# States of the samples copied through DRAM scratch beside the pair products, transposed as fp32r, and updated into their own tile

## The chip, the cores and the metric

The kernel runs on one core of one Trainium2 chip. Its engines have separate instruction streams: TensorE (PE in the profile, its weight loads PEld), VectorE (DVE), ScalarE (ACT), GpSimd (POOL) and SyncE (SP). SP and ACT also issue DMAs; SP's are on queue q1 and ACT's on queue q10. The metric is the device time of one execution in microseconds (us); the time given is the median of several runs.

## What is computed

One layer of a hybrid decoder for a prompt of 1024 tokens and for 8 samples of 8 tokens each. A projection of the normalized input feeds a pooling branch and a state-space (SSD) branch; their outputs are gated, added and projected. The change concerns the SSD branch of the samples, where each of the 32 heads has a state of 64 x 128 from an earlier step:

```python
def step(h, inp):
    xq, dq, Bq, Cq = inp
    acs = jnp.cumsum(dq * Ag, axis=1)
    ...
    y = jnp.einsum('bijge,bjgep->bigep', att, xq)
    y = y + jnp.einsum('bign,bige,bgepn->bigep', Cq, jnp.exp(acs), h)
    last = acs[:, -1]
    w_in = jnp.exp(last[:, None] - acs) * dq
    h = h * jnp.exp(last)[..., None, None] + jnp.einsum('bjgn,bjge,bjgep->bgepn', Bq, w_in, xq)
    return h, y
```

For the samples there is one such step per sample. `h` (8 samples x 32 heads x 64 x 128, 8.4 MB in float32) is an input, `state_ssm`. It is used twice: in `y`, which needs it turned (the state dimension n on the partitions), and in the new `h`, which is an output.

## The kernel before

All 1088 tokens (1024 + 64) lie on the free axis, features on the 128 partitions. Products that need float32 accuracy are made of three fp32r products of high and low parts ("whi", "wlo" are the parts of a weight tile, made by ACT at L166 and by POOL or DVE at L169).

The program has five stages on the span. Up to about 100 us the input is normalized. From 100 to 585 us come the **pair products**: `pair` makes two blocks of 128 columns of the big projection at a time by seven Strassen products (lines L609 to L611 on PE), whose raw weights are loaded on SP into a ring of five tiles named rawA (L541, L544, in `pair_w`). Beside them `splits` prepares other weights: it loads them on ACT, halves them, and stores one half on SP (L442, tiles pw to DRAM ws or wp). From about 590 to 790 us the last ten pairs run with the **samples' SSD** beside them (`ssd_samples`, called by `samples_beside`, a generator whose steps are spread evenly over the products). From 800 to 1120 us the prompt's SSD runs in chunks, beside more products, and the last stage is the output projection.

In `ssd_samples`, for each of four groups g of eight heads, the states come in eight tiles h0 of [128, 4, 128]: two heads on the partitions, four samples on the free axis. They have a ring of four buffers (`H0B`). For each half hf of the samples and each q of 0 to 3:

- `h0_load` (L1239, SP) loads one tile from `state_ssm`, in pieces of 512 bytes, three tiles ahead;
- PE turns it in four transposes against the identity `ident` (L1304), and ACT copies the result out of PSUM (L1306);
- one step later `update` makes the product for the new state on PE (L1291), DVE computes the new state in four operations **in place, into h0** (L1294), and ACT's queue stores h0 to the output (L1296). So a buffer of h0 is free for the next load only when that store has landed.

Ahead of these, each group loads its decays (dec, L1188 on SP from the DRAM tensor acs_d), which POOL masks in two operations (`far`, L1196 and L1197) and ACT puts through an exponential (L1202). The names of tiles that the views show: h is h0; hst holds the samples' x, B, C and their factors E; dec is also the name of two operands of L1291.

Before the samples, `dt_end` turns the time steps: it loads two tiles s0 and s1 from dts_d (L1090, L1091, SP) and transposes them (L1109).

What sets the order: the program is written with generators, `behind(engine)` holds an instruction back behind the last one that stands on that engine, and a scheduler then sets each engine's order within what the data and the buffers allow. An engine works through its list in order; SP's DMAs too, so that one which waits for a buffer holds back all that stand behind it.

Of the kernel before, what the change touches and what calls it, by code (L numbers as in the profile page):

```python
# [8 lines left out]
F32 = mybir.dt.float32  # L9
# [11 lines left out]
P = 128  # L21
# [4 lines left out]
NS = 64  # L26
# [20 lines left out]
def tile_pool_ssd_step(  # L47
# [6 lines left out]
    nc = tc.nc  # L54
# [41 lines left out]
    def PB():  # L96
        return psB.tile([P, 512], F32, tag="ps", name=nm("ps"))
# [19 lines left out]
    def turn_r(out, src):  # L117
        nc.tensor.transpose(out.bitcast(F32R), src.bitcast(F32R), identR)
# [272 lines left out]
    def dram(name, shape, dt=F32):  # L391
        return dr.tile(list(shape), dt, tag=name, name=name)
# [13 lines left out]
    def behind(engine, n=0):  # L406

        of = (i for i in reversed(nc.cur_bb.bb.instructions) if i.engine == engine)
        for _ in range(n):
            next(of)  # L410
        return tc.issue_after(next(of))
# [665 lines left out]
    def dt_end():  # L1077
# [7 lines left out]
        for rr in range(3):  # L1085
            nc.gpsimd.tensor_copy(blk3[32 * rr:32 * rr + 32], blk[:32, 0:4])
        F = 9 * NH
        s0 = sp.tile([P, 8 * P], F32, tag="dec", name="s0", bufs=2)
        s1 = sp.tile([P, NS], F32, tag="bt", name="s1", bufs=2)
        load(s0, dts_d[:, :SEQ])  # L1090
        load(s1, dts_d[:, SEQ:])  # L1091
# [128 lines left out]
    def spt(shape, tag, bufs, dt=F32):  # L1220
        return sp.tile(list(shape), dt, tag=tag, name=nm(tag), bufs=bufs)

    def ssd_samples(g):
        S = NS
        xb = spt([P, 6, NS], "hst", 2)
        load(xb, xbc_d[g][:, :, SEQ:])
        Bf, Cf = xb[:, 4], xb[:, 5]
        E2 = spt([P, 4, NS], "hst", 2)
        load_E(E2, g)
        dec = spt([P, 8, P], "dec", 2)[:NS, :, :NS]  # L1230
        decays(dec, g, NC)
        far(dec, NC)
        exps(dec, g, NC)
        h0s = {}

        def h0_load(j):
            hf, q = divmod(j, 4)
            h0 = spt([P, 4, P], "h0", H0B)
            load(h0, state_ssm[0, 4 * hf:4 * hf + 4, 8 * g + 2 * q:8 * g + 2 * q + 2].rearrange("b h p n -> (h p) b n"))  # L1239
            h0s[j] = h0  # L1240
        h0_load(0)
        yield
        px = PB()
        for q in range(4):
            nc.tensor.transpose(px[:S, q * P:(q + 1) * P], xb[:, q], ident)
        pc = PB()
        mm(pc[:S, :S], Bf, Cf, start=True, stop=True)
        xd = spt([P, 8, 64], "xd", 2)
        V.tensor_tensor(xd[:S], px[:S].rearrange("p (h d) -> p h d", d=64),
                        dtT[:S, NC, 8 * g:8 * g + 8].unsqueeze(2).to_broadcast([S, 8, 64]), ALU.mult)  # L1250
        V.tensor_tensor(dec, dec, pc[:S, :S].unsqueeze(1).to_broadcast([S, 8, S]), ALU.mult)
        for j in range(1, H0B - 1):
            h0_load(j)
        yield
        t = spt([P, 4, P], "xd", 2)[:, :, :NS]
        for q in range(4):
            act(t[:, q], xb[:, q], AF.Copy, scale=Dv[:, 4 * g + q:4 * g + q + 1])
        yield
        V.tensor_tensor(t, inner(xd, dec, S), t, ALU.add)
        for hf in range(2):  # L1260
            rep = spt([P, 5, 2, 3, 16], "yt", 1).rearrange("p q a r i -> p q (a r i)").rearrange(
                "p q (r i) -> p q r i", i=32)
            nc.gpsimd.tensor_copy(rep, xb[:, 0:5, 32 * hf:32 * hf + 32].unsqueeze(2).to_broadcast([P, 5, 3, 32]))
            px = PB()
            for q in range(4):
                nc.tensor.transpose(px[:96, q * P:(q + 1) * P], rep[:, q].rearrange("p r i -> p (r i)"), ident)
            pb = PB()
            nc.tensor.transpose(pb[:96, :P], rep[:, 4].rearrange("p r i -> p (r i)"), ident)
            xs = spt([P, 8, 64], "xw", 1)
            V.tensor_tensor(xs[:96], px[:96].rearrange("p (h d) -> p h d", d=64),  # L1270
                            wd3[:, hf, 8 * g:8 * g + 8].unsqueeze(2).to_broadcast([96, 8, 64]), ALU.mult)
            xh = spt([P, 512], "dec", 2, F32R)
            xsf = xs.rearrange("p h d -> p (h d)")
            act(xh[:96], xsf[:96], AF.Copy)
            V.tensor_tensor(xh[64:96], xsf[64:96], xh[64:96].bitcast(F32), ALU.subtract)
            bx = spt([P, P], "bt", 2, F32R)
            act(bx[:96], pb[:96, :P], AF.Copy)
            V.tensor_tensor(bx[32:64], pb[32:64, :P], bx[32:64].bitcast(F32), ALU.subtract)
            Bb = spt([P, 4, P], "dec", 2, F32R)
            V.tensor_tensor(Bb[:96], bx[:96].bitcast(F32).unsqueeze(1).to_broadcast([96, 4, P]),  # L1280
                            blk3.unsqueeze(2).to_broadcast([96, 4, P]), ALU.mult)
            cz = spt([P, 4, 32], "cz", 2)
            V.memset(cz, 0.0)
            V.tensor_copy(cz[:, :, 0:8], Cf[:, 32 * hf:32 * hf + 32].rearrange("p (b i) -> p b i", i=8))
            yield
            hts = {}

            def update(r):
                h0 = h0s.pop(4 * hf + r)
                pu = PB()  # L1290
                mm(pu, xh[:96, r * P:(r + 1) * P], Bb[:96].rearrange("p b n -> p (b n)"), start=True, stop=True)  # L1291
                for b in range(4):
                    cc_ = 32 * hf + 8 * b + 7
                    V.scalar_tensor_tensor(h0[:, b, :], h0[:, b, :], E2[:, r, cc_:cc_ + 1],  # L1294
                                           pu[:, b * P:(b + 1) * P], ALU.mult, ALU.add)
                store_(new_ssm_s[0, 4 * hf:4 * hf + 4, 8 * g + 2 * r:8 * g + 2 * r + 2]  # L1296
                       .rearrange("b h p n -> (h p) b n"), h0)
            for q in range(4):
                j = 4 * hf + q
                if j + H0B - 1 < 8:  # L1300
                    h0_load(j + H0B - 1)
                pt = PB()
                for b in range(4):
                    nc.tensor.transpose(pt[:, b * P:(b + 1) * P], h0s[j][:, b, :], ident)  # L1304
                hts[q] = spt([P, 512], ("hT", "yt", "hU", "hV")[q], 1)
                act(hts[q], pt, AF.Copy)  # L1306
                if q > 0:
                    update(q - 1)
                yield
            po = PB()  # L1310
            for r in (3, 0, 1, 2):
                for b in range(4):
                    mm(po[32 * b:32 * b + 32, r * P:(r + 1) * P], cz[:, b, :], hts[r][:, b * P:(b + 1) * P],
                       start=True, stop=True)
            update(3)
            yo = spt([P, 512], "hT", 1)
            act(yo, po, AF.Copy)
            yield
            pn = PB()
            for q in range(4):  # L1320
                nc.tensor.transpose(pn[:, q * P:(q + 1) * P], yo[:, q * P:(q + 1) * P], ident)
            tn = spt([P, 4, P], "yt", 1)[:, :, :32]
            V.tensor_tensor(tn.rearrange("p q (b i) -> p q b i", i=8),
                            pn.rearrange("p (q b i) -> p q b i", q=4, i=32)[:, :, :, 0:8],
                            E2[:, :, 32 * hf:32 * hf + 32].rearrange("p q (b i) -> p q b i", i=8), ALU.mult)
            th = t[:, :, 32 * hf:32 * hf + 32]
            V.tensor_tensor(th, th, tn, ALU.add)
            yield
        store_(ys_d[g], t)
# [191 lines left out]
    def run_units(units, ahead=1, beside=None):  # L1521
        pend = {}
        widx = [i for i, u in enumerate(units) if u[0] is not None]
        nxt = 0
        done_w = 0
        for i, (pf, run) in enumerate(units):
            if pf is not None:
                while nxt < len(widx) and nxt <= done_w + ahead:
                    pend[widx[nxt]] = units[widx[nxt]][0]()
                    nxt += 1  # L1530
                done_w += 1
                it = run(pend.pop(i))
                for _ in it or ():
                    if beside is not None:
                        beside()
            else:
                run(None)
        while later:
            step()

    def plain(f):
        return (None, lambda w: f())
# [41 lines left out]
    units = [plain(to_conv), light[1], plain(pool_rows)]  # L1584
    units += weave(heavy, light[2:-LAST])
    pre = splits()
    units.append(plain(lambda: [None for _ in pre]))
    units.append(plain(to_ssd))
    acc = [None] * 8
    yh, yl = [None] * NG, [None] * NG  # L1590
    run_units(units, 1, lambda: next(pre, None))
    side = iter([it for g in range(NG) for it in [ssd_samples(g)] * SSTEPS])
    due, made_ = [0.0], [0]
    FIRST = 14
# [460 lines left out]
```

## Time and profile before

| | |
|---|---|
| median of three runs | 1273.08 us (1272.99 to 1273.53) |
| the profiled execution's own time | 1271.29 us |
| its span, first to last instruction | 1269.5 us |
| PE busy | 1242.3 us, 98% of the span |
| DVE, ACT, POOL busy | 900.9, 718.0, 683.1 us |
| moved by DMA | 234.9 MB, 185 GB/s over the span |

The profile is of one execution. A line such as "L1304 PE MATMUL ps<-ident,h 128*128 128x128 f32 x4" reads: line 1304 of the kernel, on PE, writes tile ps from ident and h, 4 times in a row. In a timeline the first two numbers are start and time in us, and a bracket at the end gives idle time before and what ended it. Matmuls overlap each other: a matmul's duration says little, the distance from one start to the next says what it costs PE.

### The profile page before, as it was taken

Reading aid. Unit: us, or ns where it says so; the run is one execution under the profiler, and the core shown is the slowest. Engines: PE = TensorE matmul, PEld = TensorE weight load, DVE = VectorE, ACT = ScalarE, POOL = GpSimd, SP = SyncE. Lnnn points to the kernel's source line nnn. Section 1 sums busy time; section 2 is a strip of 40 time slices with the busy share of each in tenths; the row PEclk is TensorE's granted clock in tenths of the full one; section 3 lists DMA queues with packets and bytes.
Section 4 is the critical chain, followed back from the end, with each engine's and each line's share of the span. In section 5 each row is a group of like instructions: output and inputs, shape, how many; then the busy total and the mean of one; then the engine's idle time right before and its main releaser. Section 6 shows DMA issues by size and latency. Waiting matters only on the chain. (4 is left out here: it accounts for less than half of the span.)

```text
span 1269.5 us, 26341 instructions
## 1 busy us (share of the span) xinstructions
PE 1242.3 (98%) x9771; PEld 1173.9 (92%) x9771; DVE 900.9 (71%) x1584; ACT 718.0 (57%) x1683; POOL 683.1 (54%) x555
## 2 busy tenths in 40 slices
PE   7999999999999999999999999999999999999997
PEld 6779999999999999998989999999999999999786
DVE  4695678966979588975756665598677879766543
ACT  4665356474666656554554554687887768522211
POOL 1007669886878777764344454365565646545000
PEclk9999999999999999999999999999999999999999
DMA  9937354565456454443557445899766567485431
GB/s 332 298 104 226 116 167 161 181 204 160 138 182 201 146 182 164 149 138 116 157 142 226 151 147 167 283 300 319 217 200 201 181 212 206 152 291 179 149 108 50
DMA packets 225729, 234.90 MB, mean 185 GB/s; under 512 B 30369, under 2 KB 177009, under 8 KB 225594
## 3 DMA queue, kind: packets, MB, share of 16 engines
q1 hardware_dynamic: 155808, 159.01, 40.3%
q10 hardware_dynamic: 69794, 74.22, 17.4%
q8 instruction: 77, 1.26, 0.4%
q14 instruction: 50, 0.41, 0.1%
HBM read 158.67 MB, written 74.62 MB: 184 GB/s over the span
## 5 line engine op out<-in xcount | busy, mean ns | idle before, releaser
L169 POOL TENSOR_TENSOR wlo<-rawA,whi 128x512 fp32r<-128x512 f32 x120 | 189.0, 1580 | 170.5 <-ACT whi L166 95.8
L169 POOL TENSOR_TENSOR wlo<-raw,whi 128x512 fp32r<-128x512 f32 x92 | 155.1, 1693 | 122.2 <-ACT whi L166 119.3
L360 PE MATMUL mm<-Y,whi 128*128 128x352 f32 (+1 forms) x480 | 159.8, 333 | 0.7
L361 PE MATMUL mm<-Y,whi 128*128 128x352 f32 (+1 forms) x480 | 157.3, 328 | 0.4 <-DVE Y L1516 0.4
L362 PE MATMUL mm<-Y,wlo 128*128 128x352 f32 (+1 forms) x480 | 156.8, 327 | 0.0
L609 PE MATMUL mm<-Y,whi 128*128 128x272 f32 x496 | 146.3, 295 | 2.2 <-ACT whi L166 2.2
L611 PE MATMUL mm<-Y,wlo 128*128 128x272 f32 x496 | 143.5, 290 | 2.5 <-POOL wlo L169 2.0
L609 PE MATMUL ps<-Y,whi 128*128 128x272 f32 x496 | 143.8, 290 | 0.0
L610 PE MATMUL ps<-Y,whi 128*128 128x272 f32 x496 | 143.0, 288 | 0.0
L610 PE MATMUL mm<-Y,whi 128*128 128x272 f32 x496 | 142.9, 288 | 0.0
L611 PE MATMUL ps<-Y,wlo 128*128 128x272 f32 x496 | 142.5, 287 | 0.0
L1057 DVE SCALAR_TENSOR_TENSOR GA<-GA,cvT,GA 128x1112 f32<-128x1112 f32 x72 | 126.6, 1763 | 0.1
L166 ACT ACTIVATE whi<-rawA 128x512 fp32r<-128x512 f32 x125 | 78.1, 627 | 81.1 <-PE ps L610 44.0
L166 ACT ACTIVATE whi<-raw 128x512 fp32r<-128x512 f32 x96 | 58.9, 627 | 97.6 <-DVE raw L555 51.7
L609 PEld LDWEIGHTS mm<-Y,whi 128*128 128x128 f32 x496 | 93.5, 189 | 4.2 <-ACT whi L166 2.8
L611 PEld LDWEIGHTS mm<-Y,wlo 128*128 128x128 f32 x496 | 93.5, 189 | 2.9 <-POOL wlo L169 2.2
L360 PEld LDWEIGHTS mm<-Y,whi 128*128 128x128 f32 x480 | 90.3, 188 | 4.2 <-DVE G L1890 2.4
L610 PEld LDWEIGHTS mm<-Y,whi 128*128 128x128 f32 x496 | 93.5, 189 | 0.7 <-issue 0.6
L610 PEld LDWEIGHTS ps<-Y,whi 128*128 128x128 f32 x496 | 93.3, 188 | 0.4
L609 PEld LDWEIGHTS ps<-Y,whi 128*128 128x128 f32 x496 | 93.3, 188 | 0.2
L611 PEld LDWEIGHTS ps<-Y,wlo 128*128 128x128 f32 x496 | 93.4, 188 | 0.0
L361 PEld LDWEIGHTS mm<-Y,whi 128*128 128x128 f32 x480 | 90.3, 188 | 2.6 <-DVE Y L1516 0.9
(464 smaller groups left out, 3821.9 us busy)
## 6 DMA issues: line engine op xcount, KB each, us to landing
rawA<-in_w_in SPq DMA_DIRECT2D x46, 512.0 KB
dec<-acs_d SPq DMA_DIRECT2D x32, 512.0 KB
xbc<-GA ACTq DMA_DIRECT2D x24, 512.0 KB
xb<-xbc SPq DMA_DIRECT2D x32, 384.0 KB
rawA<-in_w_in SPq DMA_DIRECT2D x32, 256.0 KB
pw<-in_w_ssm_out ACTq DMA_DIRECT2D x32, 256.0 KB
ws<-ph ACTq DMA_DIRECT2D x32, 256.0 KB
ws<-pw SPq DMA_DIRECT2D x32, 256.0 KB
```

The source lines that it names most:

```text
L166: ins = act(hi[:, :, :ncols], raw[:, :, :ncols], AF.Copy)
L169: (eng or nc.gpsimd).tensor_tensor(lo[:, :, :ncols], raw[:, :, :ncols], hi[:, :, :ncols].bitcast(F32), ALU.subtract)
L360: mm(ps[:, :n], a, rh[k][:, o:o + n], start=(k == 0), stop=False)
L361: mm(ps[:, :n], a, rl[k][:, o:o + n], start=False, stop=False)
L362: mm(ps[:, :n], b, rh[k][:, o:o + n], start=False, stop=(k == nk - 1))
L609: mm(p, hi, ah, start=(k == 0), stop=False)
L610: mm(p, hi, al, start=False, stop=False)
L611: mm(p, lo, ah, start=False, stop=(k == 3))
L1057: V.scalar_tensor_tensor(d[:, :n], rp[:, k:k + n], cvT[:, 24 * k + mc:24 * k + mc + 1], d[:, :n], ALU.mult, ALU.add)
```

## The change

Three things are done. The 32 tiles of the states are copied by 32 DMAs from `state_ssm` to DRAM scratch `h0_d`, already in the order of a tile h0, while the pair products run (one copy in every four steps); `h0_load` then reads the scratch, 2 KB per partition in one piece. The transposes are declared fp32r, by `turn_r`, which the prompt's SSD uses already (its instruction is L118). The new state is written to a tile hn of its own, with a ring of two buffers, and stored from there. To make room, dec becomes [128, 8, 64] in place of [128, 8, 128], and s0 of `dt_end` moves from the ring dec to the ring rawA.

```diff
-        s0 = sp.tile([P, 8 * P], F32, tag="dec", name="s0", bufs=2)
+        s0 = pa.tile([P, 8 * P], F32, tag="rawA", name="s0", bufs=5)
...
-        dec = spt([P, 8, P], "dec", 2)[:NS, :, :NS]
+        dec = spt([P, 8, NS], "dec", 2)[:NS]
...
             h0 = spt([P, 4, P], "h0", H0B)
-            load(h0, state_ssm[0, 4 * hf:4 * hf + 4, 8 * g + 2 * q:8 * g + 2 * q + 2].rearrange("b h p n -> (h p) b n"))
+            load(h0, h0_d[8 * g + j])
...
                 pu = PB()
+                hn = spt([P, 4, P], "hn", 2)
...
-                    V.scalar_tensor_tensor(h0[:, b, :], h0[:, b, :], E2[:, r, cc_:cc_ + 1],
+                    V.scalar_tensor_tensor(hn[:, b, :], h0[:, b, :], E2[:, r, cc_:cc_ + 1],
...
-                       .rearrange("b h p n -> (h p) b n"), h0)
+                       .rearrange("b h p n -> (h p) b n"), hn)
...
-                    nc.tensor.transpose(pt[:, b * P:(b + 1) * P], h0s[j][:, b, :], ident)
+                    turn_r(pt[:, b * P:(b + 1) * P], h0s[j][:, b, :])
...
+    h0_d = [dram(f"h0{n}", [P, 4, P]) for n in range(32)]
+
+    def move_states():
+        for n in range(32):
+            g, hf, q = n // 8, n // 4 % 2, n % 4
+            with behind(mybir.EngineType.SP):
+                load(h0_d[n], state_ssm[0, 4 * hf:4 * hf + 4, 8 * g + 2 * q:8 * g + 2 * q + 2].rearrange("b h p n -> (h p) b n"))
+            for _ in range(4):
+                yield
+    moved = move_states()
...
-    run_units(units, 1, lambda: next(pre, None))
+    run_units(units, 1, lambda: (next(pre, None), next(moved, None)))
```

How the order of instructions moves, at three places (names end in running numbers). First on SP, where s0 and the weights of the first pair that runs beside the samples (two rawA tiles, here 7471 and 7473) are loaded; the list before, in which s0 comes seven rows after the last of these:

```order
L541 DMA rawA_6878<-in_w_in 128x4x256
L442 DMA ws_213<-pw_6727 128x512
L541 DMA rawA_7471<-in_w_in 128x4x256
L442 DMA ws_214<-pw_6864 128x512
L541 DMA rawA_7473<-in_w_in 128x4x256
L442 DMA ws_215<-pw_7039 128x512
L541 DMA rawA_7479<-in_w_in 128x4x256
```

and the changed list at the same place (the two tiles are now 7535 and 7537):

```order
L541 DMA rawA_6942<-in_w_in 128x4x256
L442 DMA ws_213<-pw_6790 128x512
L1090 DMA s_7529<-dts_d 128x1024
L442 DMA ws_214<-pw_6928 128x512
L541 DMA rawA_7535<-in_w_in 128x4x256
L442 DMA ws_215<-pw_7103 128x512
L541 DMA rawA_7537<-in_w_in 128x4x256
```

s0 now takes a buffer of the ring ahead of the two weight tiles, so each of them gets a buffer that comes free one release later. Then SP again, 14 rows later, where the first states are loaded behind a weight tile (h is h0), before:

```order
L541 DMA rawA_8541<-in_w_in 128x4x256
L1239 DMA h_1354_8161<-in_state_ssm 128x4x128
L1239 DMA h_1358_8173<-in_state_ssm 128x4x128
L1188 DMA dec_8145<-acs_d 64x8x64
L1206 DMA hst_8142<-E_d 64x4x64 x2
```

and changed:

```order
L541 DMA rawA_8609<-in_w_in 128x4x256
L1239 DMA h_1354_8225<-h_1297 128x512
L1239 DMA h_1358_8237<-h_1298 128x512
L1188 DMA dec_8209<-acs_d 64x8x64
L1206 DMA hst_8206<-E_d 64x4x64 x2
```

The places are the same, the two state loads read whole rows of the scratch. On ACT, around the exponentials of the second group's decays, before:

```order
L1257 ACTIVATE xd_8914<-hst_8846,Dv 128x64 x4
L1202 ACT_TABLE_LOAD
L1202 ACTIVATE dec_8851<-dec_8851,acT 64x64 x8
L723 DMA gp_149<-u_1430_8549 128x544
L166 ACTIVATE whi_8829<-rawA_8539 128x512
L652 ACTIVATE s_1491_8927<-mm_8931 128x272
L721 ACT_TABLE_LOAD
```

and changed:

```order
L721 ACTIVATE s_1432_8615<-s_1432_8615 128x272
L1202 ACT_TABLE_LOAD
L1202 ACTIVATE dec_8923<-dec_8923,acT 64x64
L166 ACTIVATE whi_8860<-raw_8791 128x512
L166 ACTIVATE whi_8864<-raw_8790 128x512
L1257 ACTIVATE xd_8986<-hst_8918,Dv 128x64 x2
L721 ACT_TABLE_LOAD
```

Seven of the eight exponentials now stand ahead of these rows, with a table load of their own and another one (L721) behind them, so that ACT loads its function table four times here in place of twice.

## Prediction

> **What bounds the kernel now.** I read the page's first part, then the stretches of the stages, then what PE waits for while the samples run.
>
> ```profile
> span 1269.5 us, 26341 instructions
> PE 1242.3 (98%) x9771; PEld 1173.9 (92%) x9771; DVE 900.9 (71%) x1584; ACT 718.0 (57%) x1683; POOL 683.1 (54%) x555
> ...
> q1 hardware_dynamic: 155808, 159.01, 40.3%
> ```
>
> ```profile
> 130.00:585.00 455.00, 455.00 (x3585) 448.41 (x3584) 365.08 (x557) 258.36 (x608) 344.60 (x214) 1.00 0.50 160
> 585.00:800.00 215.00, 209.13 (x1850) 200.36 (x1849) 128.52 (x330) 112.96 (x244) 96.31 (x76) 0.99 0.56 166
> ```
>
> ```profile
> PE mm L611 <- POOL wlo L169: 2.0, 1, 2.0
> ...
> PE mm L609 <- DVE u L620: 1.2, 1, 1.2
> ```
>
> PE sets the end. In the pair stage (first row: length, then PE, PEld, DVE, ACT, POOL, clock, DMA share) it is busy 455.00 of 455.00 us, so whatever the other engines and queues wait for there, it costs nothing. Beside the samples it is busy 209.13 of 215. So time can be won by taking work from PE, or a part of those 5.9 us of idleness; it can be lost by any wait that reaches PE. All of PE's waits over 1 us in that stage are single events; the two largest stand above.
>
> **The transposes.** The change replaces 128 float32 transposes.
>
> ```profile
> L1304 PE MATMUL ps<-ident,h x128: 270/272/303, 607.3 to 782.6; 128*128 128x128 f32 x128
> ```
>
> The 272 ns is a latency. The cost is the distance between starts, seen here on PE around one group of four:
>
> ```profile
> 611.51 0.29 PE L610 MATMUL ps<-G,whi 128*128 128x272 f32 x1
> 611.63 0.29 PE L611 MATMUL ps<-G,wlo 128*128 128x272 f32 x1
> 611.76 0.60 PE L1304 MATMUL ps<-ident,h 128*128 128x128 f32 x4
> 612.12 0.37 PE L609 MATMUL mm<-Y,whi 128*128 128x272 f32 x1
> 612.33 0.29 PE L610 MATMUL mm<-Y,whi 128*128 128x272 f32 x1
> ```
>
> From the first transpose to the second matmul behind them are 0.57 us; a plain step between such matmuls is 0.12 to 0.13 us (611.51, 611.63, 611.76). So four transposes add 0.57 - 0.125 = 0.445 us, 0.111 each. The same turn as fp32r runs in the prompt's chunks:
>
> ```profile
> 863.13 0.55 PE L118 MATMUL ps<-identR,xb 128*128 128x128 f32 x5
> 863.52 0.46 PE L1415 MATMUL ps<-xb 128*128 128x128 f32 x2
> ```
>
> Five in 0.39 us, 0.078 each. The difference is 0.033 us, times 128 is **4.2 us**. Bounds: at worst the pause behind a group stays (0.21 against 0.125), and only the steps shrink, 0.36 - 4 x 0.078 = 0.05 per group, times 32 is 1.5. At best an fp32r transpose costs what its 128 columns cost at the products' pace, 0.125 x 128/272 = 0.059, and (0.111 - 0.059) x 128 is 6.7. I take the middle value, since it is of the same instruction in the same kernel. Nothing hides it: the products around the transposes are PE's own.
>
> [...]
>
> **The loads of the states and the wait at 601 us.** PE's longest wait comes from POOL, which has two masks (L1196, L1197) ahead of the weight part that PE needs; the masks wait for a load of decays, that load for a store of acs_d. SP, POOL, PE and the clock:
>
> ```profile
> 589.22 1.18 SPq L1239 DMA_DIRECT2D h<-in_state_ssm  x2
> 596.41 0.62 SPq L1188 DMA_DIRECT2D dec<-acs_d  x1
> ```
>
> ```profile
> 599.64 1.10 POOL L1196 TENSOR_SCALAR_AFFINE_SELECT dec<-dec 64x512 f32<-64x512 f32 x1 [0.28 <-DMA dec<-acs_d]
> ...
> 601.87 1.25 POOL L169 TENSOR_TENSOR wlo<-rawA,whi 128x512 fp32r<-128x512 f32 x1
> ```
>
> ```profile
> 600.89 0.28 PE L610 MATMUL mm<-Y,whi 128*128 128x272 f32 x1
> 603.18 0.39 PE L611 MATMUL mm<-Y,wlo 128*128 128x272 f32 x1 [2.00 <-POOL wlo L169]
> ```
>
> ```profile
> 604.00:608.00 4.00, 4.00 (x33) 3.59 (x32) 2.57 (x5) 2.96 (x7) 0.00 (x0) 0.58 0.44 131
> ```
>
> PE stands 2.29 - 0.12 = 2.2 us, and then runs four microseconds at a clock of 0.58, which costs 4 x 0.42 = 1.7 us more: 3.9 us in all. The order of this chain is the same after the change (the rows of SP in the section on the change); only the two state loads that run while the store is under way become lighter. Queue q1 spends 40.3% of 16 x 1269.5 us on 155,808 packets of 159 MB: 0.84 us of all 16 engines for 256 KB by its bytes, 1.7 us by 512 packets at 52.5 ns. Read as 128 packets it would be 0.4 by packets. So each of the two loads may be shorter by nothing (bytes) to 1.3 us (packets). The store shares the engines with them, and I take **0.7 us** off its landing, half of what one load can give, and so off the wait; ends nothing, and 3.9 where the wait falls so low that the slow clock goes with it.
>
> **The update into hn.** DVE now must wait until the store of two updates before has landed. What that is worth can be seen, because SP waits for the same stores today:
>
> ```profile
> SPq L1239 <- DMA out<-h: 103.5, 28, 18.9
> ```
>
> ```profile
> 613.79 2.15 DVE L1294 SCALAR_TENSOR_TENSOR h<-h,hst,ps 128x128 f32<-128x128 f32 x8
> 634.17 1.12 DVE L1294 SCALAR_TENSOR_TENSOR h<-h,hst,ps 128x128 f32<-128x128 f32 x4 [0.24 <-PE ps L1291]
> ```
>
> ```profile
> 612.95 0.41 ACTq L1296 DMA_DIRECT2D out<-h  x1
> 631.22 1.41 ACTq L1296 DMA_DIRECT2D out<-h  x2
> ```
>
> ```profile
> 615.40 7.92 SPq L1239 DMA_DIRECT2D h<-in_state_ssm  x4
> 635.57 1.05 SPq L1239 DMA_DIRECT2D h<-in_state_ssm  x2
> ```
>
> The store issued at 612.95 let go of its buffer at 615.40, that of 631.22 at 635.57: 2.5 and 4.4 us. The update two later starts about 614.9 (half of the eight at 613.79) and 634.17. So DVE would be held 0.5 and 1.4 us, about 1 us in each of the eight half groups, 8 us in all. Behind it on DVE stand the additions that empty PE's banks (L620, L625). What such a hold costs PE:
>
> ```profile
> 623.73 0.44 DVE L620 TENSOR_TENSOR u<-s,mm 128x272 f32<-128x272 f32 x1 [1.84 <-DMA z<-u]
> 658.03 0.44 DVE L620 TENSOR_TENSOR u<-s,mm 128x272 f32<-128x272 f32 x1 [4.15 <-DMA gp<-u]
> ```
>
> ```profile
> 658.52 0.40 PE L609 MATMUL mm<-G,whi 128*128 128x272 f32 x1 [1.24 <-DVE u L620]
> ```
>
> A hold of 1.84 us shows no wait of PE, one of 4.15 us shows 1.24. So holds of 1 us are taken at **nothing**; without that cover they cost up to 8 us. In return SP stands 103.5 us less: the loads of h0, and the weights behind them, come earlier. That wins nothing by itself, since no wait of PE there is for a load of states or weights.
>
> **The copies, s0 and the tables, all at nothing.** The copies move 8.4 MB each way. 32 x 512 packets at 52.5 ns over 16 engines are 54 us of DMA, 12% of the 455 us in which the queues are half idle. SP issues 32 more DMAs of 0.4 to 0.6 us while its weight loads wait for buffers. The tightest place is the two weight tiles behind s0:
>
> ```profile
> 487.46 0.38 SPq L541 DMA_DIRECT2D rawA<-in_w_in  x1
> ...
> 501.57 0.38 SPq L541 DMA_DIRECT2D rawA<-in_w_in  x1
> ...
> 510.92 0.38 SPq L541 DMA_DIRECT2D rawA<-in_w_in  x1
> ```
>
> ```profile
> 515.55 0.68 DVE L555 TENSOR_TENSOR raw<-rawA,rawA 128x512 f32<-128x512 f32 x1
> ```
>
> They move from 487.46 and 501.57 to 501.57 and 510.92, and DVE reads both at 515.55. 4.6 us is about what a load of 512 KB takes (2.5 for the 256 KB above, 0.84 more by bytes, double that where DMA is half busy), so DVE may stand up to 1 us there, which by the two holds above does not reach PE; without the cover it costs 1 us. ACT's two table loads more:
>
> ```profile
> 647.36 1.28 ACT L1202 ACT_TABLE_LOAD   x1
> ```
>
> They are 2.6 us, in a stage in which ACT is busy 112.96 of 215. At nothing, ends nothing and 2.6.
>
> **Sum.** The profiled execution took 1271.29 us, 1269.5 of span and 1.8 around it; the median is 1273.08. 1271.29 - 4.2 - 0.7 = 1266.4 for such an execution; taken to the median, 1273.08 - 4.9 = **1268.2 us**.
>
> **Rivals.** (a) *The wait at 601 goes altogether*, with its slow clock: 1273.1 - 4.2 - 3.9 = 1265.0. For it: the store and the masks hang on DMAs that get lighter. Against it: masks of 1.1 us each still stand ahead of the weight part. (b) *Waits take the gain back*: the scheduler's new order and the tables hold up a whi or wlo part, 2.6 us from the tables at the worst: 1270.8, too little to tell from no change. For it: every wait of the samples' stage is a single event of 1 to 2 us, which a shifted order makes or removes. (c) *Slower: the store's landing decides.* If the holds of DVE reach PE in full (8 us), 1268.2 + 8 = 1276.2. It decides from the point where a store takes over 5 us to land, since 4.4 gave 1.4 and about 2 are covered. Against it: DVE is busy 128.52 of 215 and catches up. [...]
>
> **How the numbers follow.** Forecast 0.42, (a) 0.18, (b) 0.16, (c) 0.16, (d) 0.08. What a measurement here can tell from no change is 0.2%, 2.5 us: faster is below 1270.5, slower above 1275.6. Faster: 0.40 of the forecast, 0.18, and 0.06 of (b): 0.64. Slower: 0.15 of (c) and 0.02 for what I don't see: 0.17. The same: 0.19. The likeliest case alone spans 1266 to 1270.5 (transposes 1.5 to 6.7). The range 1262.5 to 1276 leaves out the outer half of (c), and of (a) the best transposes.
>
> **What would show it.** PE's stage beside the samples shorter by about 5 us, the pair stage unchanged at full PE; groups of four at L118 stepping 0.08 us; SP without waits for stores; DVE instead waiting for stores of hn about 1 us at a time. Wrong, if PE shows new waits on DVE behind the updates, if PE has idle time before 585 us, or if the wait at 601 grows.

## The result and the profile after

The changed kernel takes 1278.81 us (median of 7 runs, 1277.58 to 1283.89); the kernel before, 1273.08 (7 runs). The ratio is 1.0038 with a 95% interval of 1.0022 to 1.0054: about 4.8 us **slower**, where about 5 us less was forecast. The profiled execution took 1278.81 us, its span 1277.1.

The stretches that the prediction showed, now of the changed kernel (length, then PE, PEld, DVE, ACT, POOL, clock, DMA share, GB/s):

```profile
130.00:585.00 455.00, 455.00 (x3583) 447.99 (x3582) 364.34 (x556) 256.54 (x607) 345.69 (x214) 1.00 0.56 177
585.00:800.00 215.00, 206.98 (x1835) 197.55 (x1834) 133.39 (x330) 114.11 (x245) 91.57 (x74) 0.98 0.54 158
```

The pair stage is as full as before (455.00 of 455); only the DMA share rose, from 0.50 to 0.56, by the copies. Beside the samples PE is busy 206.98 us in place of 209.13, and in the same 215 us it gets through 1835 matmuls in place of 1850. In the stage behind it as many are missing, 2578 in place of 2594 (before, then changed):

```profile
800.00:1120.00 320.00, 318.22 (x2594) 300.34 (x2592) 239.95 (x376) 238.75 (x630) 175.93 (x198) 1.00 0.73 228
800.00:1120.00 320.00, 316.94 (x2578) 299.14 (x2577) 239.69 (x376) 237.02 (x623) 176.28 (x199) 0.99 0.71 227
```

What PE, DVE and SP wait for beside the samples, 585 to 800 us (waiting work, releaser: us in all, times, longest):

```profile
PE mm L609 <- ACT whi L166: 4.8, 6, 2.2
PE ps L1292 <- DVE dec L1275: 2.1, 3, 1.0
PE mm L611 <- POOL wlo L169: 0.9, 1, 0.9
```

```profile
DVE hn L1295 <- DMA out<-hn: 10.0, 4, 4.0
```

```profile
SPq L1239 <- DVE hn L1295: 92.6, 25, 17.3
```

The wait for POOL at 601 us has shrunk from 2.0 to 0.9, and the half clock behind it is gone (1.00 from 600 to 610 us). In its place PE waits 4.8 us for weight parts of ACT (before, 1.5 in two waits). SP doesn't stand less: its loads of states wait 92.6 us for the update, where they waited 103.5 for the store.

The largest new wait is at the change from the first to the second group of heads. ACT there, in the changed kernel:

```profile
641.44 1.28 ACT L1202 ACT_TABLE_LOAD   x1 [1.80 <-PE ps L610]
643.54 1.78 ACT L1202 ACTIVATE dec<-dec,acT 64x64 f32<-64x64 f32 x7 [0.81 <-POOL dec L1197]
645.34 1.28 ACT L721 ACT_TABLE_LOAD   x1
646.64 0.43 ACT L721 ACTIVATE s<-s 128x272 f32<-128x272 f32 x1
647.09 1.28 ACT L1202 ACT_TABLE_LOAD   x1
648.38 0.35 ACT L1202 ACTIVATE dec<-dec,acT 64x64 f32<-64x64 f32 x1
...
648.63 1.13 ACT L166 ACTIVATE whi<-raw 128x512 fp32r<-128x512 f32 x2
```

and in the kernel before:

```profile
644.92 1.15 ACT L166 ACTIVATE whi<-raw 128x512 fp32r<-128x512 f32 x2 [0.56 <-PE ps L611]
...
646.30 1.05 ACT L1257 ACTIVATE xd<-hst,Dv 128x64 f32<-128x64 f32 x4
647.36 1.28 ACT L1202 ACT_TABLE_LOAD   x1
648.65 0.35 ACT L1202 ACTIVATE dec<-dec,acT 64x64 f32<-64x64 f32 x1
```

Before, the two weight parts (whi, L166) stand ahead of the second group's exponentials (L1202). Now they stand behind them, with three table loads and ACT's wait for POOL's mask in between, and are made 3.7 us later. PE stops for them, and the clock halves behind the stop (same columns as the stretches above):

```profile
649.30 0.59 PE L609 MATMUL mm<-Y,whi 128*128 128x272 f32 x1 [2.16 <-ACT whi L166]
```

```profile
646.90:649.10 2.20, 0.24 (x2) 0.01 (x1) 0.28 (x1) 2.17 (x4) 0.00 (x0) 1.00 0.00 0
649.10:655.90 6.80, 6.60 (x41) 6.16 (x42) 3.04 (x6) 6.42 (x16) 6.25 (x5) 0.50 0.39 130
```

6.8 us at a clock of 0.50 cost up to 3.4. Stop and clock are 5.7 us together, as much as the medians differ by. That the two figures agree is luck, as the same two profiles show when the n-th of the 5208 matmuls of L609 to L611 in the one is compared with the n-th in the other. The changed kernel is 1.0 us behind at 595 us and 1.8 ahead at 648. It is 0.9 behind at 667, with the stop between, and 2.9 at 794. At the end it is 7.6 behind. The 4.7 us from 794 us on come from the prompt's SSD, where PE waits longer at one place (here before, then changed) and the clock halves for 3.4 us (0.50 from 830.0 us), and from another such stretch of 3.4 us at 1120 (0.51). Whether the change is behind these two is open.

```profile
825.88 0.25 PE L118 MATMUL ps<-identR,xb 128*128 128x128 f32 x1 [1.42 <-DVE btl L1444]
830.22 0.34 PE L118 MATMUL ps<-identR,xb 128*128 128x128 f32 x1 [2.06 <-DVE btl L1445]
```

So one execution doesn't settle what the order on ACT costs. The rest of this document tests it by changing the order.

The transposes themselves did get cheaper. A group of four in the changed kernel:

```profile
624.42 0.46 PE L118 MATMUL ps<-identR,h 128*128 128x128 f32 x4
624.72 0.36 PE L609 MATMUL ps<-Y,whi 128*128 128x272 f32 x1
624.91 0.29 PE L610 MATMUL ps<-Y,whi 128*128 128x272 f32 x1
```

From the first transpose to the second matmul behind are 0.49 us, against 0.57 in the group that the prediction shows: 0.07 to 0.08 less, 2.3 to 2.6 us for the 32 groups.

### The profile page after: what moved, and what is told of

Same layout as the page of the kernel before. It is cut to its first block, busy times and chain, and to the rows that moved or that the text cites. A ratio compares the mean times of both kernels' runs of the same rounds, so it can differ in the third digit from the quotient of the medians.

```text
span 1277.1 us, 26395 instructions
## 1 busy us (share of the span) xinstructions
PE 1245.8 (98%) x9771; PEld 1176.2 (92%) x9771; DVE 904.9 (71%) x1584; ACT 718.6 (56%) x1685; POOL 681.1 (53%) x555
## 5 line engine op out<-in xcount | busy, mean ns | idle before, releaser
L169 POOL TENSOR_TENSOR wlo<-rawA,whi 128x512 fp32r<-128x512 f32 x120 | 188.0, 1572 | 164.8 <-ACT whi L166 92.6
L609 PE MATMUL mm<-Y,whi 128*128 128x272 f32 x496 | 147.2, 297 | 4.2 <-ACT whi L166 4.2
L611 PE MATMUL mm<-Y,wlo 128*128 128x272 f32 x496 | 144.1, 291 | 1.4 <-POOL wlo L169 0.9
L609 PE MATMUL ps<-Y,whi 128*128 128x272 f32 x496 | 143.7, 290 | 0.0
L611 PE MATMUL ps<-Y,wlo 128*128 128x272 f32 x496 | 142.6, 287 | 0.0
L1057 DVE SCALAR_TENSOR_TENSOR GA<-GA,cvT,GA 128x1112 f32<-128x1112 f32 x72 | 129.4, 1801 | 0.1
L166 ACT ACTIVATE whi<-rawA 128x512 fp32r<-128x512 f32 x125 | 78.0, 626 | 78.1 <-PE ps L610 46.0
L166 ACT ACTIVATE whi<-raw 128x512 fp32r<-128x512 f32 x96 | 58.7, 626 | 97.1 <-DVE raw L555 45.5
L609 PEld LDWEIGHTS mm<-Y,whi 128*128 128x128 f32 x496 | 94.1, 190 | 6.4 <-ACT whi L166 5.1
L611 PEld LDWEIGHTS mm<-Y,wlo 128*128 128x128 f32 x496 | 93.9, 190 | 1.9 <-POOL wlo L169 1.1
L609 PEld LDWEIGHTS ps<-Y,whi 128*128 128x128 f32 x496 | 93.3, 188 | 0.2
L611 PEld LDWEIGHTS ps<-Y,wlo 128*128 128x128 f32 x496 | 93.4, 188 | 0.0
```

The lines of the kernel that those rows point to most:

```text
L166: ins = act(hi[:, :, :ncols], raw[:, :, :ncols], AF.Copy)
L169: (eng or nc.gpsimd).tensor_tensor(lo[:, :, :ncols], raw[:, :, :ncols], hi[:, :, :ncols].bitcast(F32), ALU.subtract)
L609: mm(p, hi, ah, start=(k == 0), stop=False)
L611: mm(p, lo, ah, start=False, stop=(k == 3))
L1057: V.scalar_tensor_tensor(d[:, :n], rp[:, k:k + n], cvT[:, 24 * k + mc:24 * k + mc + 1], d[:, :n], ALU.mult, ALU.add)
```

## The experiments

Four theories. **Order**: ACT's list, with the exponentials ahead of the weight parts, and the half clock it sets off. **Stores**: DVE's waits for the stores of hn. **Copies**: the traffic of the copies. **Boundary**, formed after the first four runs: at each change of group ACT waits for a store of ys before it can go on, whatever the list. Times are medians; the ratio is to the kernel before, run beside it on the same chip, and is what counts, since that kernel's own median went from 1273.4 to 1275.4 between the sets of runs.

| run | what it is | us | ratio (95%) |
|---|---|---|---|
| exps_later | the change, second group's exponentials held behind three weight parts (the "pin") | 1273.59 | 1.0004 (0.9987 to 1.0021) |
| copies_alone | before + copies | 1274.64 | 1.0003 (0.9989 to 1.0016) |
| own_tile_alone | before + tile hn | 1281.68 | 1.0052 (1.0032 to 1.0073) |
| plain_turns | the change, fp32 transposes | 1279.97 | 1.0040 (1.0025 to 1.0056) |
| own_out | the change, t in a ring of its own | 1269.92 | 0.9962 (0.9950 to 0.9975) |
| own_out_before | before, t in a ring of its own | 1271.12 | 0.9969 (0.9952 to 0.9985) |
| pin_plain_turns | pin, fp32 transposes | 1279.03 | 1.0038 (1.0024 to 1.0052) |
| hn4 | pin, four buffers of hn | 1268.59 | 0.9944 (0.9926 to 0.9963) |
| hn4_plain_turns | pin, four buffers, fp32 transposes | 1273.06 | 0.9988 (0.9972 to 1.0004) |
| four_tiles | the change, four buffers of hn, no pin | 1273.48 | 0.9989 (0.9971 to 1.0007) |
| ring_three | the change, t in its own ring, three buffers of hn | 1269.54 | 0.9959 (0.9942 to 0.9977) |
| pin_ring_three | the same with the pin | 1270.80 | 0.9962 (0.9944 to 0.9979) |
| hn4_old_list | hn4 with ACT's list of two buffers at one place | 1272.38 | 0.9988 (0.9973 to 1.0003) |

### The parts one by one

exps_later holds the exponentials back (`highs` is the list of the weight parts that ACT makes):

```diff
-        exps(dec, g, NC)
+        with tc.issue_after(highs[-4]) if g == 1 else ExitStack(): exps(dec, g, NC)
```

> The changed kernel (1278.8 us) with one pin: ACT's exponentials of the second group stand behind three weight parts instead of ahead of them. Order theory (ACT's list, with these exponentials and two table loads ahead of a weight part, makes PE stop 2.3 us at 647 us, and the half clock that follows costs 3.4 us): the stop and the half clock go, 1278.8 - 5.7 = 1273.1. Store theory (the stores of hn hold DVE) and copy theory (the copies' traffic): nothing to do with these exponentials, so within 1 us of 1278.8.

copies_alone is the kernel before with `h0_d`, `move_states` and `load(h0, h0_d[8 * g + j])`, and nothing else.

> The kernel before with the copies alone: states loaded from the scratch, updated in place, turned as fp32. Order theory: ACT's list is that of before, so 1273.1, up to 1 us less by the lighter loads. Store theory: no tile hn, so 1273 too. Copy theory (12% more DMA in the pair stage delays what PE waits for): 1276 or more, with idle time of PE before 585 us.

own_tile_alone is the kernel before with the tile hn, and with dec made smaller and s0 moved to make room for it:

```diff
...
+                hn = spt([P, 4, P], "hn", 2)
...
-                    V.scalar_tensor_tensor(h0[:, b, :], h0[:, b, :], E2[:, r, cc_:cc_ + 1],
+                    V.scalar_tensor_tensor(hn[:, b, :], h0[:, b, :], E2[:, r, cc_:cc_ + 1],
...
```

> The kernel before with the tile hn alone (and the tiles dec and s0 made small and moved for it): states loaded from the input, turned as fp32. Order theory: ACT's list has the exponentials of the second group ahead of the weight part, as in the change, so 1273.1 + 5.7 = 1278.8 or more, up to 1283 if all of the change's loss is in it; PE stops at about 647 us for a weight part of ACT. Store theory: the same time, but the stops come behind DVE's waits for stores of hn. Copy theory: 1273.

plain_turns is the change with `nc.tensor.transpose(..., ident)` in place of `turn_r`.

> The changed kernel with the states' transposes in fp32 (copies and hn kept). If the fp32r transposes save what their steps say (a group of four 0.30 us against 0.44, times 32): 1278.8 + 4.4 = 1283.2, by all theories of the loss. If they save nothing, or their time is taken by waits that stand beside them: 1278.8.

The copies cost nothing that can be told (0.03%, between -0.11 and 0.16): that theory falls. The pin alone brings the change back to the time before: the ratio falls by 0.0034 (between 0.0011 and 0.0057), 4.3 us. In its profile ACT makes two weight parts, and a third, ahead of the exponentials:

```profile
642.80 1.15 ACT L166 ACTIVATE whi<-raw 128x512 fp32r<-128x512 f32 x2 [0.69 <-DVE raw L555]
...
645.77 1.28 ACT L1202 ACT_TABLE_LOAD   x1
```

The tile hn alone costs 0.52%, 6.6 us, if anything more than the change as a whole, and in its ACT list the second group's exponentials stand ahead of the weight parts, as in the change. PE stops at the same place for the same reason, longer:

```profile
643.81 1.28 ACT L1202 ACT_TABLE_LOAD   x1 [2.60 <-DMA dec<-acs_d]
646.49 0.35 ACT L1202 ACTIVATE dec<-dec,acT 64x64 f32<-64x64 f32 x1 [1.39 <-POOL dec L1197]
646.85 1.28 ACT L721 ACT_TABLE_LOAD   x1
```

```profile
652.24 0.39 PE L609 MATMUL mm<-Y,whi 128*128 128x272 f32 x1 [3.91 <-ACT whi L166]
```

So the scheduler's list turns over with the tile hn, or with the two tiles that make room for it; no run separates these. In copies_alone, which has neither, the eight exponentials stand behind the two weight parts, as before. The order theory stands, and it belongs to one part of the change.

The time can be split further, roughly, since each run lists its span and mean clock; their product is taken as an estimate of the span at full clock, if PE sets the pace. Its mean is 1267.1 us for the kernel before in that set, 1271.2 for the change and 1269.3 with the pin. Of the 5.3 us between the mean times of the change (1279.3) and of the pin (1274.1), 1.9 are by this estimate time at full clock, and 3.3 the halved clock.

plain_turns was expected at 1283.2 and took 1280.0: in the change itself the cheaper transposes bring 0.02%, which can't be told from nothing (uncertainty 0.22%). (The expectation's 0.44 us for a group had the pause behind it and the 0.30 hadn't; like for like it is 0.57 against 0.49, and 2.3 us.)

### What else takes the gain

The pin leaves the kernel at 1273.6, and the transposes should have shown there. Its waits of PE and DVE:

```profile
PE mm L609 <- ACT whi L166: 4.3, 5, 2.0
PE ps L1292 <- DVE dec L1275: 2.0, 3, 1.0
PE mm L609 <- ACT s L652: 1.3, 1, 1.3
```

```profile
DVE hn L1295 <- DMA out<-hn: 11.9, 6, 3.6
```

and ACT at the change to the third group:

```profile
696.10 0.35 ACT L1257 ACTIVATE xd<-hst,Dv 128x64 f32<-128x64 f32 x1 [2.02 <-DMA ys<-xd]
...
696.93 1.28 ACT L1202 ACT_TABLE_LOAD   x1
698.23 2.02 ACT L1202 ACTIVATE dec<-dec,acT 64x64 f32<-64x64 f32 x8
700.15 0.61 ACT L166 ACTIVATE whi<-raw 128x512 fp32r<-128x512 f32 x1
```

ACT waits for the landing of the last group's output (ys), because t shares the ring xd; exponentials and a weight part stand behind. own_out and own_out_before give t a ring:

```diff
-        t = spt([P, 4, P], "xd", 2)[:, :, :NS]
+        t = spt([P, 4, NS], "ty", 2)
```

> The changed kernel with the samples' output tile t in a ring of its own (no longer in the ring xd, where ACT waits at L1257 for the landing of the store of ys, 2.0 to 2.8 us at each change of group, with the exponentials and weight parts behind it). ACT's list then has the exponentials of the second group behind two weight parts again. Order theory: as with the pin, 1273.1. Boundary theory (ACT's wait for ys at each change of group, with the exponentials behind it, is what takes the transposes' gain back): the stops of PE at about 649, 699 and 749 us shrink too, 3 us more: 1270. Store theory: 1278.8.

> The kernel before with t in a ring of its own. Boundary theory: before has the same wait of ACT, and PE's stops of 1.4 and 1.3 us at 657 and 750 us shrink: 1271 to 1272. Order theory: ACT's list changes little, 1273.6 within 1.

hn4 is the pinned kernel with `spt([P, 4, P], "hn", 4)`; pin_plain_turns the pinned kernel with fp32 transposes.

> The pinned kernel (1273.6 us) with four buffers of hn in place of two: DVE's waits for stores of hn, 11.9 us there in six waits, go. If they reach PE (store theory): PE's stops behind DVE, 0.8 and 0.6 us at 707 and 716 us and up to 3 us more, go: 1270 to 1272. If DVE makes them up (order and boundary theories): 1273.6 within 1.

> The pinned kernel (1273.6 us) with the states' transposes in fp32. If fp32r turns are worth their steps there: 1273.6 + 4.4 = 1278.0. If PE only reaches waits for ACT and DVE earlier (boundary theory): 1274 to 1275.5, and PE's stops at the changes of group are smaller by what the turns are longer.

own_out came out as the boundary theory said, 9.7 us (0.76%, by the ratios) below the change. The stops that the pinned kernel has at 701 and 752 us (1.5 and 2.3 us between two matmuls) are gone in it: from 660 to 800 us no two matmuls are more than 0.7 us apart. One stop of 2.4 us is left at 658, for DVE. PE's waits:

```profile
PE ps L118 <- DVE ty L1259: 2.1, 1, 2.1
PE mm L611 <- POOL wlo L169: 1.2, 1, 1.2
PE mm L609 <- ACT whi L166: 1.1, 2, 0.7
```

Part of it is the list again: with t in its ring the scheduler puts two weight parts back ahead of the second group's exponentials by itself. The kernel before gains too, 0.31% or 3.9 us, so this wait was there all along. pin_plain_turns says that the transposes are worth 0.34%, 4.3 us, with the pin; the interval of that difference reaches from 1.5 to 7, so the 2.3 us of the steps lie in it.

hn4 came out below what the store theory asked for (1270 to 1272): 5.0 us less than the pin by the medians and 7.6 by the ratios. DVE's waits for hn are gone from its trace. But its ACT list isn't that of the pin, either.

### Stores or list

> The changed kernel (1278.8 us) with four buffers of hn and nothing else; ACT's exponentials of the second group stay ahead of the weight parts. If the order and the holds of DVE by the stores are two costs that add up (5.2 by the pin, 5.0 by four buffers behind the pin): 1278.8 - 5.0 = 1273.8, with PE's stop at about 647 us still there. If the pin's gain came from the holds, or the other way round: 1278.8 or 1268.6.

> The kernel with the pin and four buffers of hn (1268.6 us) with the states' transposes in fp32. If the transposes are worth their steps wherever no new wait stands: 1268.6 + 4.4 = 1273.0, which is the time before. If the gain was from the waits alone: 1268.6 to 1270.

With and without four buffers, with and without the pin: 1.0038, 1.0004 (pin), 0.9989 (buffers), 0.9944 (both). The two add up, 0.3 to 0.5% for the pin and 0.5 to 0.6% for the buffers, each with about 0.25% of uncertainty. In four_tiles PE still stops at 649 us, with 1.9 us between two matmuls, and a stretch at half clock follows. The transposes are worth 0.44%, 5.6 us, beside both (interval from 2.5 to 8.7).

> The changed kernel with three buffers of hn and the output tile t in a ring of its own (1269.9 us with two buffers). If both waits count, DVE's for stores (5.7 us left there) and ACT's for ys: about 3 us less, 1267. If two buffers do with t in its ring: 1269.9 within 1.

> As the one before, and with the pin behind three weight parts. If one more weight part ahead of the exponentials helps PE at 649 us: 1 us below it; if the exponentials' delay then holds DVE and the turns: 1 us above.

ring_three is where own_out was, so with t in its ring two buffers do, although DVE waited 5.7 us for stores there. The pin on top brings nothing either: 1.3 us more by the medians, the same by the ratios. Its best case, 1 us less, missed. In its profile the pin does harm: the held exponentials come so late that PE waits 5.0 us at 654 us, with 6.8 us at half clock, so the pin is no cure in itself.

Four buffers also make the scheduler put one weight part ahead of the third group's exponentials. hn4_old_list holds that part behind them, as with two buffers; the other rows are nearly those of hn4:

```diff
...
+        h0s = g == 2 and held.append(nc.cur_bb.bb.instructions[-1]) or {}
...
-        ins = act(hi[:, :, :ncols], raw[:, :, :ncols], AF.Copy)
+        with tc.issue_after(held.pop()) if held else ExitStack(): ins = act(hi[:, :, :ncols], raw[:, :, :ncols], AF.Copy)
```

> The pinned kernel with four buffers of hn (1268.6 us), but with the exponentials of the third group ahead of the weight part again, as the list with two buffers has them (with four the scheduler puts one weight part ahead of them). If DVE's holds by the stores are what the two buffers cost: 1268.6, at most 1.3 us more for PE's stop at 699 us. If the changed list is what four buffers bring: 1273.6, the time of the pinned kernel.

It takes 1272.4, 0.9988. So of the 7.6 us (ratios) that four buffers brought behind the pin, 2.0 (between -0.8 and 4.9) are the holds themselves, and 5.6 (between 2.6 and 8.7) the one weight part's place in the list. What it does to PE doesn't stay where it is: at the change to the third group PE stops only 0.4 us (in the pin 1.3), but one group later, in hn4_old_list,

```profile
738.88 0.44 DVE L620 TENSOR_TENSOR u<-s,mm 128x272 f32<-128x272 f32 x1 [5.68 <-DMA gp<-u]
```

```profile
747.18 1.07 ACT L1257 ACTIVATE xd<-hst,Dv 128x64 f32<-128x64 f32 x4 [3.14 <-DMA ys<-xd]
748.25 1.28 ACT L1202 ACT_TABLE_LOAD   x1
749.55 1.30 ACT L1202 ACTIVATE dec<-dec,acT 64x64 f32<-64x64 f32 x5
750.76 0.61 ACT L166 ACTIVATE whi<-rawA 128x512 fp32r<-128x512 f32 x1
```

```profile
PE mm L609 <- ACT whi L166: 3.8, 3, 3.1
```

and in hn4

```profile
734.50 0.44 DVE L620 TENSOR_TENSOR u<-s,mm 128x272 f32<-128x272 f32 x1 [3.49 <-DMA gp<-u]
```

```profile
742.71 1.06 ACT L1257 ACTIVATE xd<-hst,Dv 128x64 f32<-128x64 f32 x4 [1.63 <-DMA ys<-xd]
```

DVE waits longer for a store of the products (gp), so the group's output is stored later, so ACT waits longer for it, and the weight part behind is later: PE stops 3.1 us. That DVE's longer wait comes from the moved weight part is argued, not shown.

## Why the prediction was wrong

**The transposes: the mechanism was right, the size too large.** They step at about 0.07 us; the term of 4.2 measures 2.3 by the steps, inside its bounds of 1.5 and 6.7. The 0.111 us of a float32 transpose had in it the longer step behind the group, and the 0.078 of fp32r hadn't; from the first transpose to the next matmul a group of four takes 0.355 us in float32 and 0.293 in fp32r, 0.089 and 0.073 each, so float32 doesn't step at the 0.111 that the prediction read. The longer step behind a group stays at 0.2. In whole runs it is 0.3, 4.3 and 5.6 us in three surroundings, each with about 3 us of uncertainty. The 0.08 at (d), that the steps would stay as they were, is out: they did shrink.

**The wait at 601 us: better than the 0.7 forecast.** It fell from 2.2 to 1.1 us, and in this execution no half clock followed. Whether lighter loads did it is open: in own_tile_alone, which has no copies, the same distance between two matmuls is 1.46 us, in copies_alone 1.15, in own_out_before, which has nothing of the change, 1.65, in the kernel before 2.29.

**The copies and s0 at nothing: right as far as it shows.** The copies alone are at 1.0003, and in the changed kernel PE is full in the pair stage (455.00 of 455 us), with s0 loaded in it.

**The step that failed is "ACT's two table loads ... At nothing".** It priced the moved instructions, 2.6 us in a stage in which ACT is busy 113 of 215, and not what had come to stand behind them. In ACT's list these instructions cost what they waited for as well. The exponentials wait for POOL's masks (ACT 0.81 us), these for a load of decays (POOL 5.18 us ahead of L1196), and the weight parts behind them wait along: 3.7 us late, PE stopped for 2.3 of them, and up to 3.4 more went with the clock. Rival (b) had named this very mechanism, but took 2.6 us for "the worst", left out the clock that the same prediction had charged at 601 us, and so came to "no change". With rival (b) at 5.7, its sum would have been 1273.1 - 4.9 + 5.7 = 1273.9. That is still short of 1278.8, and the runs with four buffers show a second term at nothing that was wrong.

**That second term is the ring of two for hn, "holds of 1 us are taken at nothing".** Four buffers take 6.2 us off the changed kernel (0.49%) and 7.6 off the pinned one. The holds weren't of 1 us: four waits in the change make 10.0 us, the longest 4.0. Yet in the pinned kernel the holds by themselves cost 2.0 us (between -0.8 and 4.9), and the rest goes with the place of one weight part in ACT's list. Rival (c), the store's landing decides, put the ring at 8 us and came near the right time partly by luck, since its reason carries the smaller part as far as these runs tell.

**"SP stands 103.5 us less" was wrong.** A buffer of h0 now comes free when the update has read it, and SP waits 92.6 us for the updates where it waited 103.5 for the stores.

**What was missing altogether** is that PE's stops in this stage gather at the changes of group, behind chains of waits that end in ACT's list, and that time which PE saves ahead of such a place can be waited away there. In the profiles the changed kernel is 2.0 us ahead of plain_turns at 690 us, by the count of the products of L609 to L611, and 0.3 ahead at 720, behind the change to the third group. Beside the pin and four buffers (hn4 against hn4_plain_turns) nothing is lost there: the lead is 4.7 us at 690 and 5.0 at 720. These are single executions, so the sizes are rough. None of the three signs that the prediction gave of being wrong came: PE's waits on DVE in this stage are 2.1 us (before, 2.2), PE has no idle time from 130 to 585 us, and the wait at 601 shrank.

The time that was forecast, 1268.2 us or a ratio of 0.9962, is reached with the chain cut in one place (own_out, 0.9962) or with the buffers and the pin (hn4, 0.9944, the fastest measured, 5 runs). For own_out that may be luck: own_out_before reaches 0.9969 without any of the change, so that own_out's kernel is faster by the transposes rather than by the ring of t alone can't be told. For hn4 it is better founded, since with fp32 transposes it goes back to 0.9988.

Not tried: the fp32r transposes without copies and hn, and the list of the change in the kernel before.

## What to carry to other kernels

Where a scheduler writes the lists, a change of buffers is a change of order: compare the lists, and at each place where something moved ahead of what the bounding engine needs, add up what the moved instructions wait for, not how long they take. Price a stop of the bounding engine with the slow clock that may follow it (here up to 3.4 us behind a stop of 2.3). And before counting a saving on that engine, look for the next place where it waits for another one: there the saving may end, unless that chain is shortened as well (here a ring of its own for one small tile did it).

## What was not expected of the hardware

**The half clock depends on where a stop falls.** In the profiles it comes in stretches of 3.41 us, or two in a row, which start a whole multiple of 3.413 us apart within an execution: in the changed kernel at 649.1, 830.0 and 1120.1 us, 53 and 85 multiples between them, at a clock of 0.50. Of 14 stops with 2.2 to 2.7 us between two matmuls (from 100 us on, over all 15 profiles) 7 were followed by one; of four stops of 3.4 us and more, all. Lay such a grid through an execution by one of its half-clock stretches, and add up the idle time of PE in each window of 3.41 us at full clock between 585 and 850 us. Of 12 windows with 1.85 us or more all were followed by half clock, of 7 with 1.5 to 1.8 us two, of 1128 with less none. A stop that the grid cuts in two can pass. This one in the pinned kernel, 2.1 us that the grid cuts at 750.6, does, at full clock:

```profile
749.70:751.90 2.20, 0.22 (x3) 0.01 (x1) 0.00 (x0) 2.19 (x8) 0.27 (x1) 1.00 0.00 0
751.90:755.30 3.40, 3.40 (x38) 3.19 (x39) 2.31 (x5) 3.27 (x8) 1.29 (x1) 1.00 0.03 13
```

No stop is needed. The stretch at 1120.1 us comes behind a window in which the profile has PE busy throughout, but for 2.05 us of it with 18 matmuls of a single column each:

```profile
1116.72:1120.14 3.42, 3.42 (x27) 3.39 (x26) 0.82 (x3) 1.02 (x5) 0.00 (x0) 1.00 0.55 177
```

```profile
1116.85 2.05 PE L1845 MATMUL ps<-ones,sq_acc 128*128 128x1 f32 x18
```

All 15 profiles have these 18 matmuls. In six they lie within one window, and half clock follows in all six; in nine the grid cuts them, and it follows in none.

So a stop cost its length and, where it fell badly, 1.7 or 3.4 us on top, an estimate from 3.41 and 6.83 us at a clock of 0.50. The grid lies elsewhere from one execution to another: the stretch at 603.9 us in the kernel before and that at 649.1 us in the changed one are 13.2 times 3.413 us apart. The mean clock differs from run to run of one kernel: in the 34 runs of the kernel before beside ring_three it was 0.993 to 0.999, which on 1268 us at full clock makes about 7.7 us by estimate, and those runs took 1268.85 to 1280.29 us.
